# A hybrid decoder layer on one core: feed-forward in five token blocks, with the samples in the first superblock

## The chip, the cores and the metric

The kernel runs on one core of a Trainium2 chip. The metric is device time in microseconds (us) for one execution; before the change the median of three runs is 2588.84 us (2588.73 to 2595.58).

## What is computed

One layer of a decoder for 2048 prompt tokens and 8 x 8 = 64 sample tokens that share all weights. The model width is 1024, the hidden width of the feed-forward 4096, the memory has 256 tokens. All numbers are 32-bit floats.

```
h = rmsnorm(x) ; proj = h @ w_in             # q 512, k 128, v 128, u 512
attn = window attention, window 128, sinks, ALiBi (8 heads, 2 kv heads)
pool = causal means of u over 2, 4, 8, 16 tokens, times w_pool
x = x + concat(attn, pool) @ w_out
x = x + cross(rmsnorm(x) @ w_cq, mem_k, mem_v) @ w_co      # 4 heads x 256
x = x + square(relu(rmsnorm(x) @ w_up)) @ w_down
y = rmsnorm(x)
```

The prompt's memory keys and values come from `mem_prompt @ w_ck, w_cv`, and every prompt token shares them. Each of the 8 samples has its own window cache, pooling history and memory cache (`cmk`, `cmv`: 8 MB each), so the samples need an attention and a cross stage of their own.

## The kernel before, in words

Activations are kept transposed: channels on the 128 partitions, tokens along the free axis. Every product is made with three matmuls, because each operand is split into a rounded high part and a low part: Wh x Hh, Wh x Hl, Wl x Hh (`mm3`, L109 to L114, and the same three in `dense`, L310 to L312). A weight chunk of 128 x 1024 is loaded by a DMA of SyncE (SP) into one of six staging slots `f` (L132), rounded by ScalarE (L133), and its low part is made by VectorE (L134). The class `Stream` does this in the fixed order in which the chunks will be used, ahead of use, as long as there are pairs of the twelve weight slots `w` and staging slots left. Slots of every kind are handed out first in, first out, in the order of the program's text; the toolchain then plans the order of the instructions on each engine, which can differ from the text as far as the data and the slots allow. That order is fixed when the kernel is built.

The tokens are worked on in three superblocks of two blocks each (`SBLOCKS`, L24 to L28): 384 + 384, 384 + 384, and 256 + 320, where 320 is 256 prompt tokens and the 64 samples. `dense` takes each weight chunk through both blocks.

The prologue (L391) makes the prompt's memory keys and values and folds `w_cq` into the keys (`a_s`) and `w_co` into the values (`b_s`). Results of folds pass through the staging slots to DRAM (`put_fold`, L359). Each superblock (L513) then does:

- the input projection (L864), ten chunks of both blocks, in which `in_evac` (L544) splits keys and queries and makes the pooling sums. In the first superblock only, the four folds of `w_pool` into `w_out` (`fold`, L378) stand between its first four steps; they need `wpool`, loaded and scaled in `prep_fold` (L366), again through a staging slot;
- window attention, interleaved with the rest of the projection. Each tile of 128 tokens and each kv head pass five steps (`attn_a` to `attn_pv`, from L690). In the last superblock the samples' attention (`attn_sample`, L772) comes first. From its start, that superblock keeps two staging slots for the samples' value caches (`cvs`, L534); `v32` (L523) takes one in every superblock;
- the output projection (`add_evac`, L923), the cross stage (`cross`, L946), and the product with `b_s` (`add_evac2`, L1126). In the last superblock `sample_cross` (L1001) runs beside `cross`: queries with `w_cq`, scores against 16 key tiles (L1037), softmax, 16 value tiles (L1075), and `w_co`;
- the feed-forward: `up(g)` and `down(g)` for eight groups of 512 hidden channels, in order up 0, up 1, down 0, up 2, down 1 and so on. Around down(6) and down(7), the input norms of the next superblock's two blocks are made (`norm1`, L488), four staging slots each. After down(7), `final` (L1212) norms and stores a block.

Small pieces such as norms are put in a list (`later`) and taken up by `flush` a counted number of chunk steps later.

The keys of a superblock's last 128 tokens are carried to the next one in split form by GpSimd (`kcar`, L522 and L559).

Of the kernel before, what the change touches and what calls it, by code (L numbers as in the profile page):

```python
# [14 lines left out]
P = 128  # L15
NB = 384
# [16 lines left out]
C_D, C_DS, C_RC, C_QSC, C_SLS = 0, 256, 640, 704, 708  # L33
C_N = 710
# [17 lines left out]
def kernel(ctx: ExitStack, tc: tile.TileContext, io, nW=12, nF=6, nT=8):  # L52
# [10 lines left out]
    FS = Slots([sb(f"f{i}", 1088) for i in range(nF)])  # L63
    TS = Slots([sb(f"t{i}", 400) for i in range(nT)])
    XT = [sb(f"x{i}", 3136) for i in range(2)]
# [4 lines left out]
    b_s = drp.tile([8, P, 1024], F32, name="b_s", tag="b_s")  # L70

# [11 lines left out]
    kcar = sb("kcar", 512, F32R)  # L83
# [80 lines left out]
    for s in range(3):  # L164
        for c in CIN:
            S.add(("in", s, c), io["win"][c])
            if s == 0 and c in (0, 1):
                for g in range(2):
                    S.add(("wop", 2 * c + g), io["wop"][2 * c + g])
        for c in range(8):  # L170
            S.add(("wo", s, c), io["woa"][c], wo_s[c])
        for hf in range(2):
            for kp in range(4):
                S.add(("A", s, hf, kp), a_s[hf, kp])
        for c in range(8):
            S.add(("B", s, c), b_s[c])
        for g in range(9):
            for c in range(4):
                if g < 8:
                    S.add(("up", s, g, c), io["wup"][4 * g + c])  # L180
            for c in range(4):
                if g > 0:
                    S.add(("dn", s, g - 1, c), io["wdn"][4 * (g - 1) + c])
# [79 lines left out]
    def gain(bl, act, k, g):  # L263

        gk = vec[:, g + k:g + k + 1]
        nc.scalar.activation(act.hi(k), bl.x(k), AF.Copy, scale=gk)  # L266
        nc.vector.scalar_tensor_tensor(act.lo(k), bl.x(k), gk, f32(act.hi(k)), ALU.mult, ALU.subtract)

    class Act:
        def __init__(self, n):  # L270
            self.n = n
            self.h = [ACTS.get(), ACTS.get()]
            self.l = [ACTS.get(), ACTS.get()]

        def hi(self, k, c0=0, c1=None):
            return k4(self.h[k // 4])[:, k % 4, c0:self.n if c1 is None else c1]

        def lo(self, k, c0=0, c1=None):
            return k4(self.l[k // 4])[:, k % 4, c0:self.n if c1 is None else c1]
# [8 lines left out]
    def order(nch, head, tail):  # L288
        out = []
        for lo_, hi_, outer in ((0, head, True), (head, nch - tail, False), (nch - tail, nch, True)):  # L290
            if outer:
                out += [(c, b) for b in (0, 1) for c in range(lo_, hi_)]
            else:
                out += [(c, b) for c in range(lo_, hi_) for b in (0, 1)]
        return out

    def dense(keys, blks, hi, lo, evac, head=2, tail=3, after=None, piece=8, seq=None):
# [3 lines left out]
        for c, b in seq or order(nch, head, tail):  # L301
            while fetched <= c:
                loaded[fetched] = S.next(keys[fetched])
                left[fetched] = 2
# [4 lines left out]
            for k in range(8):  # L309
# [3 lines left out]
                if k < 7 and k % piece == piece - 1:  # L313
                    yield
            evac(c, b, ps)
# [50 lines left out]
    def prep_fold():  # L366
        wpr = WS.get()
        nc.sync.dma_start(cst[:], io["cst"])
# [107 lines left out]
    def make_blks(s):  # L476
        blks = []
        off = 0
        for b, (t0, npr, ns) in enumerate(SBLOCKS[s]):
            bl = Blk()  # L480
            bl.s, bl.b, bl.t0, bl.np, bl.ns, bl.n, bl.off = s, b, t0, npr, ns, npr + ns, off
            off += npr
            bl.xt = XT[b]
            bl.x = (lambda bl: lambda k, c0=0, c1=None: bl.xt[:, 0:8 * bl.n].rearrange("p (k n) -> p k n", n=bl.n)[:, k, c0:bl.n if c1 is None else c1])(bl)
# [3 lines left out]
    def norm1(bl, wait=2):  # L488
# [5 lines left out]
        else:  # L494
            xs = [FS.get() for _ in range(4)]
            for i in range(4):
                nc.sync.dma_start(xs[i][:, 0:2 * n], io["x"][:, 8 * bl.t0 + 2 * i * n:8 * bl.t0 + 2 * (i + 1) * n])
# [12 lines left out]
    def load_x(bl):  # L510
        nc.sync.dma_start(bl.xt[:, 0:8 * bl.n], io["x"][:, 8 * bl.t0:8 * (bl.t0 + bl.n)])

    def superblock(s, blks, nxt):  # L513
        last = s == 2
        smp = blks[1] if last else None
        npt = sum(bl.np for bl in blks)
        kz = [[WS.get() for _ in range(2)] for _ in range(2)]
        for kv in range(2):
            for hl in range(2):
                i = 2 * kv + hl  # L520
                if s > 0:
                    nc.gpsimd.tensor_copy(kz[kv][hl][:, 0:P], f32(kcar[:, i * P:i * P + P]))  # L522
# [6 lines left out]
        if last:  # L529
# [14 lines left out]
        def in_evac(c, b, ps):  # L544
            bl = blks[b]
            n = bl.n
            if c == 0:
                for kv in range(2):
                    r = slice(64 * kv, 64 * kv + 64)
                    o = slice(64 - 64 * kv, 128 - 64 * kv)  # L550
                    d = slice(P + bl.off, P + bl.off + bl.np)
                    src = ps[r, 0:bl.np]
                    rnd(src, kz[kv][0][r, d], kz[kv][1][r, d])
                    nc.scalar.copy(kz[kv][0][o, d], src)
                    nc.vector.tensor_tensor(kz[kv][1][o, d], src, f32(kz[kv][0][r, d]), ALU.subtract)
                    if b == 1 and not last:
                        for hl in range(2):
                            i = 2 * kv + hl
                            nc.gpsimd.tensor_copy(kcar[:, i * P:i * P + P], f32(kz[kv][hl][:, P + npt - P:P + npt]))  # L559
                if smp is bl:  # L560
                    t = TS.get()
                    nc.vector.tensor_copy(t[:, 0:192], ps[:, bl.np - P:n])
                    nc.sync.dma_start(io["wkp"], t[:, 0:P])
                    nc.sync.dma_start(io["wks"][:, :, 120:128], t[:, P:192].rearrange("p (b t) -> p b t", t=8))
                    for kv in range(2):
                        r = slice(64 * kv, 64 * kv + 64)
                        nc.gpsimd.tensor_copy(kS[r, kv, :], t[r, P:192])
                        nc.sync.dma_start(io["wks"][r, :, 0:120], ckz[r, :, kv, 8:P])
                    TS.put(t)
            elif c == 1:  # L570
                nc.vector.tensor_copy(v32[:, bl.off:bl.off + n], ps[:, 0:n])
                if smp is bl:
                    nc.sync.dma_start(io["wvp"], v32[:, npt - P:npt])
            elif c < 6:
                j = c - 2
                if last and (c, b) == (2, 0):
# [7 lines left out]
                if smp is bl:  # L584
                    nc.vector.tensor_scalar(
# [98 lines left out]
        cp = Slots(TS2)  # L684
# [87 lines left out]
        def attn_sample():  # L772
# [3 lines left out]
            dsm = cst[:, C_DS:C_DS + 384].rearrange("p (g s) -> p g s", s=192)  # L776
# [25 lines left out]
            TS.put(qf)  # L802
            nc.vector.tensor_scalar(t[:, 8:12], t[:, 0:4], -1.0, None, ALU.mult)
# [46 lines left out]
        if last:  # L850
# [25 lines left out]
        def attn():  # L876
# [11 lines left out]
            if last:  # L888
# [34 lines left out]
        def add_evac(c, b, ps):  # L923
            bl = blks[b]
            nc.vector.tensor_tensor(bl.x(c), ps[:, 0:bl.n], bl.x(c), ALU.add)  # L925
            gain(bl, bl.h2, c, V_GCROSS)
# [19 lines left out]
        def cross():  # L946
# [13 lines left out]
            for hf in range(2):  # L960
                A = [S.next(("A", s, hf, kp)) for kp in range(4)]
                for bl in blks:
# [23 lines left out]
                    if hf == 1:  # L986
                        bl.h2.free()
# [5 lines left out]
        def load_split(src):  # L993
            r, th, tl = FS.get(), ACTS.get(), ACTS.get()
            nc.sync.dma_start(r[:, 0:1024], src)
            nc.scalar.copy(th[:, 0:1024], r[:, 0:1024])
            nc.vector.tensor_tensor(tl[:, 0:1024], r[:, 0:1024], f32(th[:, 0:1024]), ALU.subtract)
            FS.put(r)
            return th, tl

        def sample_cross():  # L1001
            bl = smp
            q0, q1 = AUX.get(), AUX.get()
            qq = [q0, q1]
            for k in range(8):
                w = load_split(io["wcq"][k])
                for i in range(2):
                    mm3(qq[i][0:64, :], [k], lambda k: bl.h2.hi(k, bl.np, bl.n), lambda k: bl.h2.lo(k, bl.np, bl.n),
                        lambda k: w[0][:, 512 * i:512 * i + 512], lambda k: w[1][:, 512 * i:512 * i + 512], k == 0, k == 7)
                ACTS.put(*w)  # L1010
            yield
# [3 lines left out]
            AUX.put(q0, q1)  # L1015
            qt = AUX.get()
# [3 lines left out]
            qzc = [FS.get(), FS.get()]  # L1020
            for bg in range(2):
                nc.gpsimd.memset(qzc[bg][:, 0:1024], 0.0)
                qv = qzc[bg][:, 0:1024].rearrange("p (i x) -> p i x", x=P)
                for b in range(4):
                    nc.vector.tensor_copy(qv[:, :, 40 * b:40 * b + 8], qt[:].rearrange("p (i n) -> p i n", n=64)[:, :, 32 * bg + 8 * b:32 * bg + 8 * b + 8])
            AUX.put(qt)
            yield
            sp = AUX.get()
            for bg in range(2):
                qv = qzc[bg][:, 0:1024].rearrange("p (i x) -> p i x", x=P)  # L1030
                for b in range(4):
                    for hh in range(2):
                        kk = FS.get()
                        nc.sync.dma_start(kk[:, 0:1024], io["cmk"][4 * bg + b, hh])
                        for i in range(4 * hh, 4 * hh + 4):
                            h, db = i // 2, i % 2
                            nc.tensor.matmul(sp[32 * h:32 * h + 32, 256 * bg:256 * bg + 256], qv[:, i, 32 * b:32 * b + 32],  # L1037
                                             kk[:, 256 * (i % 4):256 * (i % 4) + 256], start=b == 0 and db == 0, stop=b == 3 and db == 1,
                                             tile_position=(0, 32 * h))
                        FS.put(kk)  # L1040
                    yield
            FS.put(*qzc)
# [9 lines left out]
            for g in range(2):  # L1052
                nc.gpsimd.tensor_scalar(pp[:, 256 * g:256 * g + 256], pp[:, 256 * g:256 * g + 256], t[:, 6 + g:7 + g], 1.0, ALU.mult, ALU.mult)
            st.put(t)
            ptz = [FS.get(), FS.get()]
            for bg in range(2):
                nc.gpsimd.memset(ptz[bg][:, 0:1088], 0.0)
# [316 lines left out]
```

## Time and profile before

| what | value |
|---|---|
| median of three runs | 2588.84 us |
| the profiled run | 2594.3 us |
| its span, first to last instruction | 2592.5 us |
| mean granted TensorE clock | 0.995 |
| 114 to 317 us | first superblock: input projection, attention, output projection |
| 460 to 926 us | inside the first superblock's feed-forward |
| 2020 to 2131 us | cross stages of the third superblock |
| DMA, all queues | 244.75 MB |

In the rows of the stages the columns are the window, its length, then the busy time and the number of instructions of PE (TensorE's matmuls), PEld (its weight loads), DVE (VectorE), ACT (ScalarE) and POOL (GpSimd), the granted clock, the share of the DMA engines' time, and GB/s. In rows of single instructions the first two numbers are start and duration. Rows of groups give the count, the busy time, the mean duration in ns, and the idle time before them with what ended it. Matmul records overlap, so a matmul's price is the distance from its start to the next one's.

### The profile page before, as it was taken

What the parts mean: (1) busy time and instruction counts of PE and PEld (TensorE: products, weight loads), DVE (VectorE), ACT (ScalarE), POOL (GpSimd) and SP (SyncE); (2) the same over time, 40 slices, a digit from 0 to 9 for tenths busy, and PEclk for the clock granted to TensorE, in tenths of its full rate; (3) what the DMA queues carried; (4) which work ended last, traced back from release to release, by engine and by line L of the source; (5) the groups of instructions that cost most, each with busy time, mean ns of one, the idle gap of its engine ahead of it and who ended that gap; (6) DMA issues with size and microseconds to landing.
All of it is one profiled execution on the core that took longest, in us unless ns stands there. A gap on an engine that the chain in (4) does not pass through costs nothing. (4 is left out here: it accounts for less than half of the span.)

```text
span 2592.5 us, 38981 instructions
## 1 busy us (share of the span) xinstructions
PE 2554.5 (99%) x15775; PEld 2459.0 (95%) x15775; DVE 1385.8 (53%) x2632; ACT 997.9 (38%) x1923; POOL 175.8 (7%) x298
## 2 busy tenths in 40 slices
PE   9899999999999999999999999999999999999998
PEld 8798989999999999998999999999999769999998
DVE  8568545434444367954454344445767446444444
ACT  6666343322222244843332222223456444322331
POOL 0015010000000001421000000000022010000000
PEclk9999999999999999999999999999999999999999
DMA  7833212221211123141111222112424573222210
GB/s 282 261 124 102 88 37 78 66 65 66 65 59 64 58 65 122 40 140 57 66 62 61 65 65 66 60 59 65 141 74 143 196 277 112 83 82 82 82 58 37
DMA packets 92538, 244.75 MB, mean 94 GB/s; under 512 B 16773, under 2 KB 31557, under 8 KB 91205
## 3 DMA queue, kind: packets, MB, share of 16 engines
q1 hardware_dynamic: 92356, 242.25, 28.4%
q8 instruction: 124, 2.03, 0.3%
q14 instruction: 58, 0.47, 0.1%
HBM read 219.53 MB, written 22.69 MB: 93 GB/s over the span
## 5 line engine op out<-in xcount | busy, mean ns | idle before, releaser
L310 PE MATMUL mm<-act,w 128*128 128x384 f32 (+2 forms) x2784 | 900.4, 323 | 1.7 <-ACT act L664 1.6
L312 PE MATMUL mm<-act,w 128*128 128x384 f32 (+2 forms) x2784 | 895.8, 322 | 1.0 <-DVE w L134 0.9
L311 PE MATMUL mm<-act,w 128*128 128x384 f32 (+2 forms) x2784 | 895.9, 322 | 0.7 <-DVE act L665 0.5
L133 ACT CAST w<-f 128x1024 fp32r<-128x1024 f32 x330 | 346.0, 1050 | 828.9 <-PE mm L113 499.0
L112 PE MATMUL mm<-act,w 128*128 128x384 f32 (+2 forms) x1728 | 552.4, 320 | 3.6 <-DVE t L417 2.4
L114 PE MATMUL mm<-act,w 128*128 128x384 f32 (+2 forms) x1728 | 548.8, 318 | 1.4 <-DVE w L134 1.4
L113 PE MATMUL mm<-act,w 128*128 128x384 f32 (+2 forms) x1728 | 548.6, 317 | 0.0
L310 PEld LDWEIGHTS mm<-act,w 128*128 128x128 f32 x2784 | 525.9, 189 | 5.9 <-ACT act L664 1.9
L311 PEld LDWEIGHTS mm<-act,w 128*128 128x128 f32 x2784 | 525.8, 189 | 5.9 <-issue 2.1
L312 PEld LDWEIGHTS mm<-act,w 128*128 128x128 f32 x2784 | 525.6, 189 | 2.1 <-DVE w L134 1.8
L134 DVE TENSOR_TENSOR w<-f,w 128x1024 fp32r<-128x1024 f32 x330 | 402.7, 1225 | 129.4 <-ACT w L133 127.4
L1199 DVE TENSOR_TENSOR x<-mm,x 128x384 f32<-128x384 f32 (+2 forms) x384 | 200.0, 522 | 326.4 <-PE mm L114 326.4
L112 PEld LDWEIGHTS mm<-act,w 128*128 128x128 f32 x1728 | 327.1, 189 | 5.3 <-issue 2.6
L114 PEld LDWEIGHTS mm<-act,w 128*128 128x128 f32 x1728 | 326.9, 189 | 1.8 <-DVE w L134 1.8
L113 PEld LDWEIGHTS mm<-act,w 128*128 128x128 f32 x1728 | 326.9, 189 | 1.1
L1165 DVE SCALAR_TENSOR_TENSOR t<-mm,t 128x384 f32<-128x384 f32 (+1 forms) x192 | 100.6, 524 | 285.7 <-PE mm L312 285.7
L1166 ACT ACTIVATE t<-t 128x384 f32<-128x384 f32 (+1 forms) x192 | 95.0, 495 | 251.4 <-DVE t L1165 251.4
L1169 DVE TENSOR_TENSOR act<-t,act 128x384 fp32r<-128x384 f32 (+1 forms) x192 | 100.1, 521 | 103.9 <-ACT act L1168 103.9
L112 PE MATMUL mm<-w,act 128*128 128x512 f32 x288 | 115.0, 403 | 1.9 <-ACT w L133 1.8
L113 PE MATMUL mm<-w,act 128*128 128x512 f32 x288 | 113.6, 395 | 1.6 <-DVE w L134 1.6
L114 PE MATMUL mm<-w,act 128*128 128x512 f32 x288 | 113.3, 394 | 0.0
L266 ACT ACTIVATE act<-x,vec 128x384 fp32r<-128x384 f32 (+2 forms) x96 | 56.3, 587 | 111.1 <-DVE x L925 57.5
(200 smaller groups left out, 2040.6 us busy)
## 6 DMA issues: line engine op xcount, KB each, us to landing
f<-in_wup SPq DMA_DIRECT2D x96, 512.0 KB, 3.5
f<-in_wdn SPq DMA_DIRECT2D x96, 512.0 KB, 3.4
f<-in_win SPq DMA_DIRECT2D x30, 512.0 KB, 3.7
f<-a_s SPq DMA_DIRECT2D x24, 512.0 KB, 4.2
f<-b_s SPq DMA_DIRECT2D x24, 512.0 KB, 4.3
x<-in_x SPq DMA_DIRECT2D x6, 1536.0 KB, 7.7
f<-in_wco SPq DMA_DIRECT2D x16, 512.0 KB, 5.4
f<-in_cmk SPq DMA_DIRECT2D x16, 512.0 KB, 4.5
```

What stands on the lines that cost most here:

```text
L112: nc.tensor.matmul(ps, Wh(k), Hh(k), start=first and i == 0, stop=False)
L113: nc.tensor.matmul(ps, Wh(k), Hl(k), start=False, stop=False)
L114: nc.tensor.matmul(ps, Wl(k), Hh(k), start=False, stop=final and i == last)
L133: nc.scalar.copy(th[:], r[:, 0:1024])
L134: eng.tensor_tensor(tl[:], r[:, 0:1024], f32(th[:]), ALU.subtract)
L310: nc.tensor.matmul(ps[:, 0:n], w8(th)[:, k, :], hi(b, k), start=k == 0, stop=False)
L311: nc.tensor.matmul(ps[:, 0:n], w8(th)[:, k, :], lo(b, k), start=False, stop=False)
L312: nc.tensor.matmul(ps[:, 0:n], w8(tl)[:, k, :], hi(b, k), start=False, stop=k == 7)
L1165: nc.vector.scalar_tensor_tensor(r[:, 0:n], ps[:, 0:n], 0.0, bl.r3[:, 0:n], ALU.max, ALU.mult)
L1166: nc.scalar.activation(q[:, 0:n], r[:, 0:n], AF.Square)
L1169: nc.vector.tensor_tensor(lo, q[:, 0:n], f32(hi), ALU.subtract)
L1199: nc.vector.tensor_tensor(bl.x(m), ps[:, 0:n], bl.x(m), ALU.add)
```

## The change

The superblocks are now 256 + 320, 384 + 384, 384 + 384, with the samples in the first. In its feed-forward, the first superblock takes both its blocks' 512 prompt tokens as one block (`FB`), so 512 columns per matmul; up to there, and in the cross stage, its blocks stay 256 and 320 wide. The 64 samples do not go through that feed-forward. Their cross stage is a generator (`side`) of which one step is taken after each of the 64 chunk steps of that feed-forward; it takes `w_cq` and `w_co` from the common stream, one key or value tile a step, each loaded one step ahead. Its result goes to DRAM (`x_s`), and 16 samples are added to each of the four later blocks when these load `x`: their feed-forward and final norm are 400 wide. The feed-forward thus runs in five blocks of 512, 400, 400, 400 and 400 tokens.

With it go: keys are carried in unsplit form by VectorE and split again at the next superblock's start (`put_k`), on ScalarE and VectorE; the copies of h2 that `side` reads are made by GpSimd; the number of staging slots stays six (1024 columns for 1088), that of weight slots twelve; in the first superblock the next input norms start one flush after their loads instead of two, and both its blocks' `final` come after the last step of down(7).

```diff
-    [(0, 384, 0), (384, 384, 0)],
-    [(768, 384, 0), (1152, 384, 0)],
-    [(1536, 256, 0), (1792, 256, 64)],
+    [(0, 256, 0), (256, 256, 64)],
+    [(512, 384, 0), (896, 384, 0)],
+    [(1280, 384, 0), (1664, 384, 0)],
 ]
+NS = 16
+SO = 46
...
+    SIDE = {**{k: ("sq", k) for k in range(8)}, **{SO + k: ("so", k) for k in range(8)}}
...
+                        if s == 0 and step in SIDE:
+                            n2, k = SIDE[step]
+                            S.add((n2, k), io["wcq" if n2 == "sq" else "wco"][k])
+                        step += 1
...
+        def put_k(src, kv, d):
+            r = slice(64 * kv, 64 * kv + 64)
+            o = slice(64 - 64 * kv, 128 - 64 * kv)
+            rnd(src, kz[kv][0][r, d], kz[kv][1][r, d])
+            nc.scalar.copy(kz[kv][0][o, d], src)
+            nc.vector.tensor_tensor(kz[kv][1][o, d], src, f32(kz[kv][0][r, d]), ALU.subtract)
...
-        last = s == 2
-        smp = blks[1] if last else None
+        last, has = s == 2, s == 0
+        smp = blks[1] if has else None
...
-        if last:
+        if has:
+            ds_ = cp.get()
+            nc.sync.dma_start(ds_[:, 0:384], io["cst"][:, C_DS:C_ALL])
...
+            for j in range(16):
+                fetch("cmk", j + 1)
...
+                kk = ahead.popleft()
...
+            for j in range(4):
+                nc.sync.dma_start(x_s[j], bl.xv[:, :, bl.np + NS * j:bl.np + NS * j + NS])
...
-        if last:
-            mix(cross(), sample_cross(), 1, 2)
-        else:
-            run(cross())
+        run(cross())
+        side = sample_cross() if has else iter(())
...
+            if not has or bl.b == 0:
+                fb = FB()
+                fb.parts, fb.n = [], 0
+                fbs.append(fb)
+            bl.fb, bl.fo = fb, fb.n
+            fb.parts.append(bl)
+            fb.n += bl.nf
...
         def up(g):
-            run(dense([("up", s, g, c) for c in range(4)], blks,
...
+            for _ in dense([("up", s, g, c) for c in range(4)], fbs,
...
+                           head=2 if g == 0 else 0, tail=0, early=has and g == 0):
+                next(side, None)
...
-            norm1(nxt[0])
+            norm1(nxt[0], 1 if has else 2)
         down(6)
         if nxt is not None:
-            norm1(nxt[1])
+            norm1(nxt[1], 1 if has else 2)
         down(7)
+        run(side)
```

More of the change, by code (lines that the diff above doesn't have):

```diff
@@ L15 @@
 P = 128
-NB = 384
+NB = 400
 SEQ = 2048
@@ L286, with order @@
         pass
-    def order(nch, head, tail):
+    class FB:
+        pass
+    def order(nch, head, tail, nb=2):
         out = []
@@ L1026, in sample_cross, with fetch @@
             AUX.put(qt)
+            ahead = deque()
+            def fetch(name, i):
+                if i < 16:
+                    t = FS.get()
+                    nc.sync.dma_start(t[:, 0:1024], io[name][i // 2, i % 2])
+                    ahead.append(t)
+            fetch("cmk", 0)
             yield
             sp = AUX.get()
[L1029 to L1041, printed above, removed]
```

324 lines of the change are left out of this document (178 added, 146 removed).

## The prediction

> **What bounds the kernel now.** I read the page first, then the busy time by stage, then single matmuls in order of time.
>
> ```profile
> span 2592.5 us, 38981 instructions
> PE 2554.5 (99%) x15775; PEld 2459.0 (95%) x15775; DVE 1385.8 (53%) x2632; ACT 997.9 (38%) x1923; POOL 175.8 (7%) x298
> ```
>
> ```profile
> 460.00:926.00 466.00, 466.00 (x2689) 465.73 (x2688) 192.26 (x287) 125.78 (x193) 0.00 (x0) 1.00 0.20 63
> 926.00:992.00 66.00, 66.00 (x377) 65.20 (x376) 54.32 (x104) 27.71 (x52) 1.40 (x4) 1.00 0.29 93
> 992.00:1120.00 128.00, 125.77 (x756) 119.02 (x755) 108.16 (x278) 84.23 (x212) 45.97 (x64) 1.00 0.27 93
> 1183.00:1330.00 147.00, 146.68 (x771) 133.49 (x770) 71.91 (x128) 58.62 (x119) 11.18 (x24) 1.00 0.19 62
> 2020.00:2131.00 111.00, 109.22 (x704) 73.86 (x702) 47.05 (x104) 41.84 (x80) 12.26 (x22) 1.00 0.69 241
> ```
>
> TensorE is the bound nearly everywhere. Busy time cannot show whether it runs at its full rate, because records overlap; the distance between starts can. In the feed-forward (460 to 926) 2689 matmuls of 384 columns take 466 us, 0.1733 us each, without a gap. For other widths I take first and last starts of unbroken runs:
>
> ```profile
> 2179.73 0.28 PE L310 MATMUL mm<-act,w 128*128 128x256 f32 x1
> ...
> 2182.25 0.31 PE L310 MATMUL mm<-act,w 128*128 128x320 f32 x1
> ...
> 2185.78 0.28 PE L310 MATMUL mm<-act,w 128*128 128x256 f32 x1
> ```
>
> ```profile
> 1190.01 0.39 PE L113 MATMUL mm<-w,act 128*128 128x512 f32 x1
> ...
> 1194.32 0.39 PE L114 MATMUL mm<-w,act 128*128 128x512 f32 x1
> ```
>
> 21 matmuls of 256 lie between the first two rows: 0.120 us each; then 24 of 320: 0.147; 19 of 512: 0.227. All four widths fit 0.417 ns a column plus a fixed 13.3 ns. So a token block less saves one fixed part per matmul, and gaps outside the feed-forward are what can be lost.
>
> **Part 1, five blocks for six.** A block has 1536 feed-forward matmuls (up 32 chunks x 8 x 3, down 64 x 4 x 3). Before, one of each block costs 4 x 0.1733 + 0.120 + 0.147 = 0.960 us. After, one of 512 and four of 400 (13.3 ns + 400 x 0.417 ns = 0.180): 0.947. 1536 x 0.0133 = **-20.5 us**, all on the path, since these stages have no gaps. Nothing else gets cheaper: the in, out and cross stages keep their six blocks and widths, only in another order. Evacuation in the wide block is two VectorE pieces of 256 per chunk; with the split of a weight it stays far under the 24 x 0.227 = 5.4 us of a step.
>
> The Trainium skill, page "TensorE: Matmul & The Clock Gate", section "Back-to-back issue gap", gives a warm matmul N/2.4 ns plus about 2.5 ns. By it this part would be worth 1536 x 2.5 ns = 3.8 us, an estimate; the rows above differ, and I go by them.
>
> **Part 2, the sample cross stage moved.** It ran beside the cross stage of the third superblock; now it runs one step per chunk in the first feed-forward. TensorE is full in both places, so its work is only carried over.
>
> ```profile
> L1037 PE MATMUL aux<-f,f 128*32 128x256 f32 x128 | 11.6, 384 | 0.4 <-DMA f<-in_cmk 0.4
> L1075 PE MATMUL aux<-f,f 128*32 128x256 f32 x128 | 9.4, 388 | 1.2 <-DMA f<-in_cmv 1.2
> ```
>
> ```profile
> 2075.23 1.06 PE L1037 MATMUL aux<-f,f 128*32 128x256 f32 x8
> 2076.22 0.50 PE L113 MATMUL mm<-w,act 128*128 128x512 f32 x1
> 2076.56 0.39 PE L114 MATMUL mm<-w,act 128*128 128x512 f32 x1
> ...
> 2092.36 0.64 PE L1075 MATMUL aux<-f,f 128*32 128x256 f32 x8 [1.19 <-DMA f<-in_cmv]
> 2092.93 0.50 PE L114 MATMUL mm<-w,act 128*128 128x512 f32 x1
> ```
>
> A single key tile (eight records, two heads) takes 2076.22 - 2075.23 = 0.99 us, a value tile (four heads) 0.57. One tile per step makes 16 x 0.99 = 15.8 us of keys for 11.6, and 9.1 of values for 9.4: +4. The matmul after each of the 32 groups takes 0.34 for 0.227: +3.5. Against that, the old stage goes: of the 111 us, 288 matmuls of 512 make 65.4, about 98 of 256 11.8, keys and values 21, transposes about 6: some 7 us are lost there. In the second superblock, without samples, 288 x 0.227 + 425 x 0.1733 + 48 transposes at about 0.11 leave 2.7 of 147 lost, so for two thirds of its tiles 1.8: -5. Together **+2** (bounds -3 and +10, the latter if the tiles, fetched only one step ahead, came late). The weight splits are as many as before; they now lie in the stream.
>
> **Part 3, the opening of the first superblock.** This is the dearest new thing. Weights, the pooled-weight matrix and the fold results all pass through the six staging slots `f`, handed out in turn. The next view is the DMA queue of SyncE, then TensorE.
>
> ```profile
> 122.32 0.34 SPq L370 DMA_DIRECT2D f<-in_wpool  x1
> 122.76 0.38 SPq L132 DMA_DIRECT2D f<-in_win  x1
> 123.23 0.38 SPq L132 DMA_DIRECT2D f<-in_wop  x1
> 127.50 0.93 SPq L363 DMA_DIRECT2D wo_s<-f  x2
> 130.78 0.34 SPq L132 DMA_DIRECT2D f<-in_wop  x1
> 131.73 0.91 SPq L363 DMA_DIRECT2D wo_s<-f  x2
> 135.49 0.34 SPq L132 DMA_DIRECT2D f<-in_win  x1
> ```
>
> ```profile
> 113.96 0.34 PE L310 MATMUL mm<-act,w 128*128 128x384 f32 x1
> ...
> 125.54 0.50 PE L112 MATMUL mm<-w,w 128*128 128x512 f32 x1 [2.71 <-ACT w L373]
> ...
> 141.73 0.33 PE L310 MATMUL mm<-act,w 128*128 128x384 f32 x1
> ```
>
> ```profile
> L133 ACT CAST w<-f 128x1024 fp32r<-128x1024 f32 x330 | 346.0, 1050 | 828.9 <-PE mm L113 499.0
> L134 DVE TENSOR_TENSOR w<-f,w 128x1024 fp32r<-128x1024 f32 x330 | 402.7, 1225 | 129.4 <-ACT w L133 127.4
> ...
> f<-in_win SPq DMA_DIRECT2D x30, 512.0 KB, 3.7
> ...
> wo_s<-f SPq DMA_DIRECT2D x8, 256.0 KB, 3.8
> ```
>
> Four chunk steps and four folds lie between 113.96 and 141.73: 27.8 us for 96 x 0.1733 + 24 x 0.227 = 22.1 of work. Already now `wpool` waits for a slot until 122.32, and loads follow slots. The change takes two more slots here (`cvs`, the sample value caches, 1 MB) ahead of `wpool`; with `v32` three are held until the sample attention is done, and three go round. By the order of gets and puts, the slot of `wpool` passes to the second input chunk, and the slot of the first fold result passes in turn to the third pool-output row, the fourth, and the third input chunk. Each load holds it for 3.7 + 1.05 + 1.23 = 6.0 us. `wpool` lands behind 1 MB more, at about 127 (125.1 before); the first fold result is away at about 132; three times 6.0 gives 150 for the third input chunk, where TensorE was at 141.7. The four steps are also 96 x 0.1733 - 48 x (0.120 + 0.147) = 3.8 us shorter here (that work returns later), so the loss grows by 8.5 + 3.8, with about 1 for a longer idle gap: **+13**. Lower bound 0 (the planner finds other work or an earlier load; a gain has no mechanism), upper bound +18.
>
> **Part 4, the rest.** Sample attention moves along with the narrow blocks, at its old price, and the third superblock gets the shape of the second: 0. Where the first superblock meets the second, down(6) and down(7) last 8 x 5.44 = 43.5 us for 66, while VectorE keeps both input norms. Its 54.3 + 108.2 = 162.5 us over 194 (84%) become:
>
> ```profile
> L1199 DVE TENSOR_TENSOR x<-mm,x x384: 410/557/558, 526.7 to 2581.8; 128x384 f32<-128x384 f32 x128, 128x256 f32<-128x256 f32 x32, 128x320 f32<-128x320 f32 x32
> L1216 DVE SCALAR_TENSOR_TENSOR x<-x,vec,t x48: 479/609/619, 989.3 to 2588.6; 128x384 f32<-128x384 f32 x32, 128x320 f32<-128x320 f32 x8, 128x256 f32<-128x256 f32 x8
> ```
>
> 32 residual adds at 0.410 for 0.557, 14 norm adds likewise, 16 final scalings at 0.479 for 0.609: 9 less; the key carry, now on ScalarE and VectorE: 1.5 more. 155 over 171.5 is 90%. Bounds 0 (only order) and +13 (84% again: 184.5); I take **+4**, nearer to zero, as the norms can start early.
>
> The tail: the last scalings and adds are 400 wide for 256.
>
> ```profile
> 2581.42 0.74 DVE L1199 TENSOR_TENSOR x<-mm,x 128x256 f32<-128x256 f32 x2
> ...
> 2585.84 3.25 DVE L1216 SCALAR_TENSOR_TENSOR x<-x,vec,t 128x256 f32<-128x256 f32 x8
> ```
>
> About a dozen VectorE steps in chain, each 0.15 us longer, and some 0.4 us on the other engines, less 0.7 for which the add now waits behind the other block's scalings: **+1.5**.
>
> **Sum:** -20.5 + 2 + 13 + 4 + 1.5 = 0. The profiled run took 2594.3 us, 1.8 beside its span and 5.5 above the median of 2588.84; the difference is applied to the median: **2589 us**. About 0.3%, 7.8 us, can be told from no change.
>
> **The rivals.**
> Faster: the opening and the seam stay hidden, because loads reach their slots earlier than my chain has them. For it: `wpool` is late by 2.7 us only. Against it: the chain is one slot's reuse, which no order can shorten. -20.5 + 2 + 1.5 + about 4 = -13: 2576. Chance 0.33.
> Slower: VectorE becomes the bound at the seam. It decides as soon as the two input norms run into the second superblock's evacuations, that is if VectorE cannot exceed its 84%: +13 for +4 makes 2598; with the upper bound of the opening, 2603. For it: 90% is above any stretch quoted. Against it: feed-forward stretches before it leave VectorE idle. Chance 0.25.
> Slower, by a smaller fixed part: the weight load of each matmul lies beneath its neighbour; if it is that which holds back the narrow widths, and wide matmuls of the feed-forward's operands (the 512 row has activations stationary) gain only a fifth of the 13.3 ns, the first part saves 4 and the time is 2606. The rule of the Trainium skill in "TensorE: Matmul & The Clock Gate", section "Back-to-back issue gap", would come out there too. The straight line through 256, 320 and 384, with the very operands of the feed-forward, speaks against it: 0.03.
> My forecast, gain and new losses cancelling: 0.39.
>
> **How the numbers follow.** Faster 0.33, same 0.39, slower 0.28. The range goes from 2574, just past the first rival, to 2604, past the second; what lies outside is a gain without losses (-19) and both upper bounds with the last rival.
>
> **What would show it.** Steps right: feed-forward starts 0.227 apart in the wide block and 0.180 in the others; third input chunk of the first superblock near 150 us; key groups of 0.99 us among them. Wrong: that chunk near 140, or gaps in the first feed-forward at `cmk`/`cmv` loads, or gaps of over 10 us in all after the first seam.

## The result and the profile after

The changed kernel takes **2626.74 us** (median of 4 runs, 2626.09 to 2627.73) against 2588.78 (2586.76 to 2595.58) for the kernel before on the same chip: ratio **1.0142, 95% interval 1.0124 to 1.0161**. It is slower by 38 us, outside the predicted range. Its profiled run took 2626.8 us with a span of 2624.9, 32.4 more than the span of the profiled run before (which lay 5.5 above its own median). The top of the page after:

```profile
span 2624.9 us, 35890 instructions
PE 2569.3 (98%) x14239; PEld 2396.3 (91%) x14239; DVE 1382.9 (53%) x2646; ACT 989.9 (38%) x1931; POOL 174.2 (7%) x300
```

TensorE has 1536 matmuls fewer, as the change meant it to have, and is busy for 15 us more. That contradiction is the first thing to explain, and busy time cannot do it. The stages can, each from its first matmul to the first of the next (us, worked out from the matmuls' starts; "in" holds the input projections and the attention, "cross" the cross scores and their projection). A feed-forward is counted here, and below, to the start of its last group of three matmuls, which leaves out 0.5 to 0.7 us ahead of the next superblock; the tail runs from there to the end of the span:

| stage | before: 1st, 2nd, 3rd superblock | after | after less before, sum |
|---|---|---|---|
| prologue | 114.0 | 111.0 | -3.0 |
| in | 132.1, 123.5, 108.8 | 136.9, 132.3, 123.6 | +28.4 |
| output projection | 71.1, 67.6, 53.6 | 54.8, 68.5, 69.5 | +0.5 |
| cross | 139.6, 139.6, 146.3 | 95.6, 141.6, 141.6 | -46.7 |
| feed-forward | 534.5, 534.2, 414.1 | 407.3, 561.9, 564.4 | +50.8 |
| tail | 12.4 | 15.0 | +2.5 |

The superblocks have other sizes now, so only sums compare. The samples' cross stage has left the cross column and entered the feed-forward one, so these two belong together: +4.1, where the prediction had -20.5 + 2. The stretch of the second superblock's feed-forward after, in the view of busy time by stage (length, TensorE busy and its records, clock, DMA share, GB/s), corresponds to the 460 to 926 row of before:

```profile
1160.00:1660.00 500.00, 500.00 (x2744) 1.00 0.19 61
```

500 us for 2744 matmuls are 182.2 ns each, at a full clock and without a gap. The prediction's line gives 180.0 for 400 columns.

The rows that follow name lines of the changed kernel: L115 to L117 and L325 to L327 are the matmuls, L136 and L137 make the high and the low part of a weight, L388 and L391 load and scale the pooling weights, L571 loads the value caches, L1252 is the residual add, L1080 a key tile's matmuls.

The opening of the first superblock: the waits of TensorE between 110 and 160 us (waiting line, releaser, us, times, longest), the DMA queue of SyncE, and the first matmul of the third input chunk:

```profile
PE mm L115 <- ACT w L391: 7.4, 1, 7.4
PE mm L325 <- ACT w L136: 4.0, 2, 3.1
PE mm L327 <- DVE w L137: 1.7, 3, 0.8
```

```profile
117.71 1.91 SPq L571 DMA_DIRECT2D f<-in_cvz  x2
119.71 0.39 SPq L388 DMA_DIRECT2D f<-in_wpool  x1
...
126.70 0.33 SPq L135 DMA_DIRECT2D f<-in_win  x1
...
144.22 0.82 SPq L135 DMA_DIRECT2D f<-in_win  x2
```

```profile
148.92 0.41 PE L325 MATMUL mm<-act,w 128*128 128x320 f32 x1 [3.06 <-ACT w L136]
```

The loads of the value caches stand ahead of `wpool`, and the third chunk is loaded at 144.2 and used at 148.9: the predicted chain, with the predicted 150.

The seam to the second superblock: TensorE's waits from 800 to 830 us, busy time by stage on both sides of it (TensorE, weight loads, VectorE, ScalarE, GpSimd, then the clock), SyncE's loads of the next input weights and VectorE's splits of them:

```profile
PE mm L327 <- DVE w L137: 4.8, 1, 4.8
PE mm L325 <- DVE x L1252: 1.0, 1, 1.0
```

```profile
780.00:807.00 27.00, 27.00 (x119) 21.85 (x117) 25.42 (x57) 17.07 (x34) 0.00 (x0) 1.00 0.39 129
807.00:835.00 28.00, 22.20 (x110) 21.50 (x111) 22.06 (x46) 9.29 (x18) 0.65 (x3) 0.88 0.41 139
```

```profile
792.91 24.82 SPq L135 DMA_DIRECT2D f<-in_win  x9
```

```profile
812.71 4.63 DVE L137 TENSOR_TENSOR w<-f,w 128x1024 fp32r<-128x1024 f32 x4
```

VectorE is 94% busy ahead of the seam, then TensorE stands still and four splits come in a row. This picture fits two causes: VectorE is full, or the splits were asked for too late. The clock column shows a second cost: from 814 to 819 us TensorE is working again, busy for all 5 us, and its granted clock is 0.50.

The samples' key tiles inside the first feed-forward, TensorE in order of time:

```profile
490.31 0.39 PE L327 MATMUL mm<-act,w 128*128 128x512 f32 x1
490.63 1.06 PE L1080 MATMUL aux<-f,x 128*32 128x256 f32 x8
491.63 0.50 PE L325 MATMUL mm<-act,w 128*128 128x512 f32 x1
491.97 0.40 PE L326 MATMUL mm<-act,w 128*128 128x512 f32 x1
```

The group is 1.00 us long, as priced. But it costs on both edges: the matmul ahead of it takes 0.32 us to the group's start and the one behind it 0.34, each for 0.227.

### The profile page after: what moved, and what is told of

It is laid out like the page before. It is cut to its first block, busy times and chain, and to the rows that moved or that the text cites. A ratio compares the mean times of both kernels' runs of the same rounds, so it can differ in the third digit from the quotient of the medians.

```text
span 2624.9 us, 35890 instructions
## 1 busy us (share of the span) xinstructions
PE 2569.3 (98%) x14239; PEld 2396.3 (91%) x14239; DVE 1382.9 (53%) x2646; ACT 989.9 (38%) x1931; POOL 174.2 (7%) x300
## 4 chain that ended last, share of the span: by engine, by line
PE 88%; DVE 4%; ACT 3%; DMA 2%; POOL 2%; issue 1%; SPq 0%; DVEq 0%; ACTq 0%; POOLq 0%
PE mm L327 16%; PE mm L325 16%; PE mm L326 16%; PE mm L115 12%; PE mm L117 12%; PE mm L116 12%; DVE w L137 1%; PE aux L739 1%; POOL t L658 1%; DMA f<-in_wco 1%; ACT x L751 1%; PE aux L770 1%; ACT w L136 1%; PE aux L1080 1%; PE aux L984 1%
## 5 line engine op out<-in xcount | busy, mean ns | idle before, releaser
L325 PE MATMUL mm<-act,w 128*128 128x400 f32 (+4 forms) x2528 | 863.7, 342 | 6.0 <-ACT w L136 4.0
L327 PE MATMUL mm<-act,w 128*128 128x400 f32 (+4 forms) x2528 | 859.4, 340 | 8.5 <-DVE w L137 8.5
L326 PE MATMUL mm<-act,w 128*128 128x400 f32 (+4 forms) x2528 | 860.5, 340 | 0.0
L136 ACT CAST w<-f 128x1024 fp32r<-128x1024 f32 x346 | 363.2, 1050 | 910.6 <-PE mm L116 501.9
L115 PE MATMUL mm<-act,w 128*128 128x400 f32 (+2 forms) x1472 | 509.1, 346 | 4.0 <-DVE t L435 2.3
L117 PE MATMUL mm<-act,w 128*128 128x400 f32 (+2 forms) x1472 | 509.6, 346 | 1.9 <-DVE w L137 1.9
L116 PE MATMUL mm<-act,w 128*128 128x400 f32 (+2 forms) x1472 | 507.2, 345 | 0.0
L325 PEld LDWEIGHTS mm<-act,w 128*128 128x128 f32 x2528 | 478.3, 189 | 27.6 <-ACT w L136 7.4
L327 PEld LDWEIGHTS mm<-act,w 128*128 128x128 f32 x2528 | 480.7, 190 | 20.2 <-DVE w L137 9.6
L326 PEld LDWEIGHTS mm<-act,w 128*128 128x128 f32 x2528 | 478.4, 189 | 11.7
L137 DVE TENSOR_TENSOR w<-f,w 128x1024 fp32r<-128x1024 f32 x346 | 422.6, 1226 | 114.1 <-ACT w L136 105.9
L1252 DVE TENSOR_TENSOR x<-mm,x 128x400 f32<-128x400 f32 (+1 forms) x384 | 195.1, 521 | 348.8 <-PE mm L117 346.3
L115 PEld LDWEIGHTS mm<-act,w 128*128 128x128 f32 x1472 | 276.4, 188 | 22.7 <-issue 3.7
L117 PEld LDWEIGHTS mm<-act,w 128*128 128x128 f32 x1472 | 277.9, 189 | 13.6 <-DVE w L137 2.3
L116 PEld LDWEIGHTS mm<-act,w 128*128 128x128 f32 x1472 | 276.3, 188 | 10.1
L1216 DVE SCALAR_TENSOR_TENSOR t<-mm,t 128x400 f32<-128x400 f32 (+1 forms) x192 | 97.8, 523 | 344.5 <-PE mm L327 344.4
L1217 ACT ACTIVATE t<-t 128x400 f32<-128x400 f32 (+1 forms) x192 | 91.8, 493 | 215.1 <-DVE t L1216 215.1
L1220 DVE TENSOR_TENSOR act<-t,act 128x400 fp32r<-128x400 f32 (+1 forms) x192 | 97.4, 520 | 76.6 <-ACT act L1219 76.5
L115 PE MATMUL mm<-w,act 128*128 128x512 f32 x288 | 114.9, 402 | 3.2 <-ACT w L136 1.7
L117 PE MATMUL mm<-w,act 128*128 128x512 f32 x288 | 113.1, 393 | 0.0
L272 ACT ACTIVATE act<-x,vec 128x384 fp32r<-128x384 f32 (+3 forms) x96 | 56.4, 588 | 118.2 <-DVE x L956 61.0
```

Source lines behind the costliest of these rows:

```text
L115: nc.tensor.matmul(ps, Wh(k), Hh(k), start=first and i == 0, stop=False)
L116: nc.tensor.matmul(ps, Wh(k), Hl(k), start=False, stop=False)
L117: nc.tensor.matmul(ps, Wl(k), Hh(k), start=False, stop=final and i == last)
L136: nc.scalar.copy(th[:], r[:, 0:1024])
L137: eng.tensor_tensor(tl[:], r[:, 0:1024], f32(th[:]), ALU.subtract)
L325: nc.tensor.matmul(ps[:, 0:n], w8(th)[:, k, :], hi(b, k), start=k == 0, stop=False)
```

## The experiments

What I held after reading the two traces: the loss has four separate places. The matmuls are slower because the rows of the activation tensors moved from 384 to 400 columns apart (**layout**); the opening loses to the value caches' slots; the seam loses to late splits; the samples' steps lose at their edges. The rivals were one common bound (VectorE or the DMA queue) or the new order of work. The kernel before took 2590.8 to 2593.3 us as a median beside these runs, so the verdict on an edit is read from the length of its stage, with the time beside it.

**Matmuls alone.** No diff: groups of 24 matmuls in the kernel's order, at several widths and distances between rows.

> This kernel leaves out the whole layer and runs only groups of 24 matmuls (128x128 weights, the order high-high, high-low, low-high over eight rows), 144 of them for each of 17 combinations of width and of the distance from one row to the next in the moving tensor, nothing else beside them on any engine. Layout theory (the spacing of a matmul depends on where its moving rows lie, not only on its width): 384 columns with rows 384 apart 173 ns each, the same 384 columns with rows 400 apart 175 to 177 ns; 400 columns with rows 400 apart 182 ns, and between 179 and 181 ns at one of the distances 416, 448 or 512. Rival one (the width alone, with the neighbours of the whole kernel as the disturbance): 384 columns 173 ns at both distances, and 400 columns one number at every distance. Rival two (the clock or traffic in the changed kernel, not the instruction): 173 and 180 ns throughout here, where nothing else runs.

TensorE, the second group's first row and the last row of four cases; 119 matmuls lie between each two. In turn: 384 columns with rows 384 apart, 384 with rows 400 apart, 400 with rows 400 apart, 400 with rows 512 apart.

```profile
50.95 0.33 PE L85 MATMUL q<-act,w 128*128 128x384 f32 x1
...
71.58 0.33 PE L87 MATMUL q<-act,w 128*128 128x384 f32 x1
...
76.05 0.33 PE L85 MATMUL q<-act,w 128*128 128x384 f32 x1
...
97.00 0.34 PE L87 MATMUL q<-act,w 128*128 128x384 f32 x1
...
101.66 0.34 PE L85 MATMUL q<-act,w 128*128 128x400 f32 x1
...
123.35 0.34 PE L87 MATMUL q<-act,w 128*128 128x400 f32 x1
...
180.38 0.34 PE L85 MATMUL q<-act,w 128*128 128x400 f32 x1
...
201.80 0.34 PE L87 MATMUL q<-act,w 128*128 128x400 f32 x1
```

20.63, 20.95, 21.69 and 21.42 us over 119: 173.4, 176.1, 182.3 and 180.0 ns. Nothing else runs and the granted clock is 1.00, so both rivals fall. The 180.0 of the prediction's line exists, but at rows 512 (or 448) apart; 416 apart gave 182.2 like 400. At 256 columns it went the other way (120.0 with 384, 118.3 with 400), and 320 did not move (146.7 both).

**The kernel before with rows 400 apart, and its control.**

```
-NB = 384
+NB = 400
```

> The kernel before with only the rows of its activation tensors moved from 384 to 400 columns apart; blocks, order and samples stay. To make room some buffers are packed otherwise, which its control does as well. Layout theory: every 384-wide matmul that reads such rows takes 2 to 3 ns more, some 10,000 of them, so 18 to 26 us slower than the control, 2608 to 2615. Rival (the loss comes with the new order of work): no more than 2 us from the control.

> Control of the one above: the kernel before with the same packing of its small buffers and its rows still 384 apart. All theories: 2588, within 3 us of the kernel before.

2609.1 us (ratio to the kernel before 1.0068, 1.0053 to 1.0083) against 2592.62 for the control (1.0002, 0.9993 to 1.0012): **16.5 us for the layout alone**, a little under the expected 18 to 26; the 256-wide matmuls gain: the third superblock's feed-forward went from 414.1 to 409.0, the first's from 534.5 to 543.0. The stretch of 460 to 926 us, the kernel with 400 first, its control second:

```profile
460.00:926.00 466.00, 466.00 (x2646) 465.73 (x2645) 188.46 (x279) 120.91 (x183) 0.00 (x0) 1.00 0.18 62
```

```profile
460.00:926.00 466.00, 466.00 (x2691) 466.00 (x2690) 193.71 (x290) 125.94 (x194) 0.00 (x0) 1.00 0.18 62
```

Both are busy for all 466 us. Only the count of records tells them apart: 45 fewer matmuls were done in the same time.

**The changed kernel with rows of up to 384 columns 384 apart.**

```
-    def k4(t, n=NB):
-        return t[:, 0:4 * NB].rearrange("p (k n) -> p k n", n=NB)[:, :, 0:n]
+    def k4(t, n=384):
+        return t[:, 0:4 * 384].rearrange("p (k n) -> p k n", n=384)[:, :, 0:n]
...
-            self.w = NB if n <= NB else 512
+            self.w = 384 if n <= 384 else NB if n <= NB else 512
```

> The changed kernel with the rows of all activation tensors of at most 384 columns 384 apart again; only the 400-wide feed-forward of the second and third superblock keeps 400. Layout theory: the 384-wide groups of input, output, combined and last cross projections win 2.8 ns a matmul, the cross scores some 4, together 8 to 11 us, 2616 to 2619. Rival (the width or the order of work): 2626, within 2 us.

2619.59 us (1.0111, 1.0091 to 1.0131), span 2615.8: 7 us back by the median and 9 by the span, for the 8 to 11 that the layout theory gave (its four runs lie between 2613.8 and 2622.4). The cross stages of the second and the third superblock are 139.6 again, for 141.6.

**Weights of the seam loaded early.**

```
-        S.resF = 4 if nxt is not None else 0
+        S.resF = 0 if nxt is None or has else 4
+        if has:
+            S.resW = 4
```

> The changed kernel in which the last two down-projections of the first superblock no longer keep four staging slots free: the weights of the second superblock's first input projections may be loaded and split as soon as a slot and a pair of weight buffers is free (four buffers kept for the keys). Theory (the 1.2 and 5.0 us that TensorE stands still at 806.7 and 808.9 us come from splits that start late because of the reservation): both gone, 5 to 7 us faster, 2620 to 2622. Rival (VectorE is the bound there, 95% busy over 780 to 817 us, and splits that start earlier only push its other work later): 0 to 2 us, 2625 to 2627, with the same idle time of TensorE behind another wait on VectorE.

2618.07 us (1.0096, 1.0081 to 1.0111); "in" of the second superblock 123.5 for 132.3, **8.8 us**, the length it had before the change, and more than the 5 to 7 expected. The first input weights are loaded 8.4 us earlier, and no wait of TensorE is left from 800 to 835 us:

```profile
784.53 32.73 SPq L135 DMA_DIRECT2D f<-in_win  x9
```

```profile
780.00:807.00 27.00, 27.00 (x119) 22.14 (x119) 26.32 (x59) 17.37 (x36) 0.00 (x0) 1.00 0.33 118
807.00:835.00 28.00, 28.00 (x159) 27.82 (x158) 26.40 (x56) 12.61 (x25) 0.65 (x3) 1.00 0.51 172
```

VectorE is busier than in the changed kernel, 97% ahead of the seam and 94% behind it, and costs nothing. So it was not the bound; the reservation of four staging slots was, and the rival falls. The expectation had priced the waits alone, 5.8 us. The granted clock, 1.00 here and 0.88 in the same row of the changed kernel, accounts for most of the rest: 5 us of work at 0.50 lose an estimated 2.5 us. (The four weight buffers that the edit keeps free instead are those that the next superblock's keys take.)

**The sample values loaded after the folds.**

```
-            cvs = [FS.get(), FS.get()]
-            for i in range(2):
-                nc.sync.dma_start(cvs[i][:, 0:1024], io["cvz"][:, 1024 * i:1024 * (i + 1)])
...
+        if has:
+            for i in range(2):
+                c = FS.get()
+                cvs.append(c)
+                nc.sync.dma_start(c[:, 0:1024], io["cvz"][:, 1024 * i:1024 * (i + 1)])
...
         S.resW = RW
```

> The changed kernel in which the two staging slots for the samples' cached values, and their two loads, are taken after the four folds instead of at the first superblock's start. Theory (the opening loses some 10 us because the pooling weights and the first input chunks queue for staging slots that the values hold): TensorE's 7.6 us at 117.8 us shrink to under 3, the third input chunk is used before 145 us, 7 to 11 us faster, 2616 to 2620. Rival (the loss there is the samples' added work in the first attention, or traffic on the queue whatever holds the slots): 0 to 3 us.

2613.56 us (1.0085, 1.0067 to 1.0103); "in" of the first superblock 125.3 for 136.9 and its output projection 53.2 for 54.8: **13.2 us**, more than the 7 to 11 expected. SyncE's queue, TensorE's wait for the pooling weights, and the third input chunk's first matmul:

```profile
119.66 0.35 SPq L388 DMA_DIRECT2D f<-in_wpool  x1
120.11 0.39 SPq L135 DMA_DIRECT2D f<-in_win  x1
...
133.69 3.67 SPq L135 DMA_DIRECT2D f<-in_win  x3
...
143.59 2.73 SPq L906 DMA_DIRECT2D f<-in_cvz  x2
```

```profile
PE mm L115 <- ACT w L391: 4.8, 1, 4.8
```

```profile
140.53 0.39 PE L325 MATMUL mm<-act,w 128*128 128x256 f32 x1 [1.46 <-ACT w L136]
```

The load of `wpool` starts no earlier (119.66 for 119.71), and TensorE still waits 4.8 us for it, not under 3: here only the megabyte ahead of it is gone. The larger part comes with the slots, as predicted: the second chunk is loaded 6.6 us earlier, the third at 133.7 for 144.2, and used 8.4 us earlier. The granted clock is higher as well, 0.93 from 110 to 160 us, where it was 0.86 in the changed kernel and 0.97 in the kernel before.

**Two tiles to a step.** The old cross stage had taken two tiles at a time; this undoes the "small steps" of the change, and puts the heads in turn. The cut shows the key tiles; the value tiles are paired likewise, and as there are 16 steps fewer, `w_co` stands 16 steps sooner in the stream.

```
-            for j in range(16):
-                fetch("cmk", j + 1)
+            for j in range(0, 16, 2):
...
-                for i in range(4 * hh, 4 * hh + 4):
+                for i in (0, 2, 4, 6, 1, 3, 5, 7):
...
+                fetch("cmk", j + 2)
+                fetch("cmk", j + 3)
```

> The changed kernel in which the samples' cross stage inside the first feed-forward takes two key tiles, or two value tiles, to a step: eight matmuls of all four heads instead of four, and 16 steps fewer. The next two tiles are fetched once the two are used, so no more slots are held. Theory (each step costs its switch, some 0.3 us, and a key tile's four matmuls of two heads take 0.99 us where a value tile's of four heads take 0.57): 16 switches by 0.3 us and 16 tiles by 0.4 us, 9 to 12 us faster, 2615 to 2618. Rival one (matmuls of the four heads do not run side by side, only switches are saved): 4 to 5 us, 2622. Rival two (the fetches then come late): no faster, and TensorE waits for a key tile.

2609.63 us (1.0068, 1.0053 to 1.0083); the first feed-forward 394.8 for 407.3: **12.5 us**, just over what both parts of the theory give, so both rivals fall. By the starts of the groups, 16 x 0.99 us of keys and 16 x 0.57 of values became 16 x 1.00, 9.0 less, and 16 pairs of edges went. The time fell by 17, more than the 9 to 12 expected; what is more than the stage's 12.5 is spread over places that the edit does not touch, by at most 1.2 us each (14.9 in the span), and over what single executions differ by. TensorE in order of time:

```profile
489.75 0.39 PE L327 MATMUL mm<-act,w 128*128 128x512 f32 x1
490.07 1.07 PE L1080 MATMUL aux<-f,x 128*32 128x256 f32 x16
491.07 0.50 PE L325 MATMUL mm<-act,w 128*128 128x512 f32 x1
```

Two key tiles (16 records, four heads) take the 1.00 us that one (8 records, two heads) took. The Trainium skill, page "TensorEngine Tiling (Array Packing)", section "Key Properties", says that tiles work in parallel and that changing the tiling mode drains TensorE. The trace agrees with the first: 16 records in the time of 8. At the edges it shows a loss, 0.09 us ahead of each of the 32 groups of the changed kernel and 0.11 us behind; that this is a drain no run here shows.

**The four together.** No new edit.

> The changed kernel with the four edits together: rows 384 apart outside the feed-forward, the seam's loads free, the values late, two tiles to a step. If the four losses are separate places on TensorE's path they add: 7 (measured) + 6 + 9 + 10 = 32 us, 2594, and up to 2600 where one of them hides another. Rival (one common bound, VectorE or the DMA queue, behind all of them): over 2608.

2585.77 us (0.9979, 0.9970 to 0.9988), better than expected; the rival of one common bound falls. The four spans taken back one by one are 9.1 + 8.7 + 12.8 + 14.9 = 45.5 us; together they give 40.7 (2624.9 - 2584.3), so they are separate places but for 5 us. Of these, 1.8 are counted twice, since the layout edit also shortened "in" of the second superblock (130.5 for 132.3) and the seam edit alone already brings it to 123.5, the four together to 123.3; and 2.5 lie in the prologue (113.5 for 111.0), whose length went from 110.2 to 113.5 us over these runs; why stays open.

**Where rows begin.** A second kernel of matmuls alone.

> This kernel too leaves out the whole layer and only runs groups of 24 matmuls, 96 for each case. First two rows in turn, the second 0 to 56 columns behind a multiple of 64, widths 400, 384 and 256; then the kernel's own pattern at 400 columns in rows 400 apart with the low rows turned by 0 to 3 places in their tile, with the eight rows taken in order or 0, 4, 1, 5, 2, 6, 3, 7, and with the low row second or third of its three matmuls; last the cross scores' 512-wide matmul with its weights read from rows 384 or 400 apart. Theory (what counts is where a row begins against where the last one was, in columns modulo 64): with both rows on multiples of 64 the line of the run before, 180 ns at 400 and 173 at 384; with other distances up to 8 ns more or less, the same for all pairs of one distance, and one of the sixteen orders of the pattern within 0.5 ns of 180 or below. Rival one (a row that does not begin on a multiple of 64 costs 2 ns whatever came before): 182 in all sixteen orders, and 182 where both rows begin 16 columns behind a multiple. Rival two (the pitch itself): two rows in turn show the line at every distance. For the weights read from rows 400 apart: 231 ns if the loss of the cross scores is theirs, 227 if not.

Each row is one case of 96 matmuls of 400 columns: two rows in turn on multiples of 64 columns; the kernel's pattern; the same with the low rows two places further in their tile.

```profile
49.87 17.53 PE L78 MATMUL q<-act,w 128*128 128x400 f32 x96
...
424.40 17.74 PE L78 MATMUL q<-act,w 128*128 128x400 f32 x96
...
459.56 17.63 PE L78 MATMUL q<-act,w 128*128 128x400 f32 x96
```

0.21 and 0.10 us over 95 distances: 2.2 and 1.1 ns a matmul above the first case, which from first to last group runs at 180.0. Among the two-row cases the second row 8, 16, 32 or 40 columns off gave 183.3, 181.7, 181.6 and 180.8; among the sixteen patterns the values lay between 180.9 and 182.4. So rivals one and two fall: neither a fixed price for a row off the multiples of 64 nor the pitch explains these; the same rows in another order cost another time. My own rule in its simple form falls as well. Both rows 16 off: 180.0, as it should be; but both 32 or both 48 off: 183.4, though their distance is a multiple of 64; and no order of the pattern came within 0.5 ns of 180.0. Which addresses meet badly stays open. The cross scores' matmul, with its weights read from rows 384 and 400 apart, took 226.7 and 231.7 ns: that part of the cross stages' 2 us is the weights' layout, not the moving rows'.

**The four and the low rows turned.**

```
         def lo(self, k, c0=0, c1=None):
-            return self.at(self.l, k, c0, c1)
+            return self.at(self.l, k ^ 2 if self.w == NB else k, c0, c1)
```

> The kernel of the four edits with one more: in the 400-wide feed-forward the low rows lie two places further in their tile (row k in place k exclusive-or 2), nothing else. Theory (the spacing follows where the rows begin; the pattern alone measured 181.0 ns so, 182.2 as they lay): 6,144 matmuls by 1.15 ns, 7 us faster, 2579; the feed-forward of the second and the third superblock 3.5 us shorter each, 558 and 561 us. Rival (in the whole kernel evictions and loads beside the matmuls hide or change this): no more than 2 us, 2584 to 2586.

**2581.91 us, ratio 0.9960 (0.9947 to 0.9974)**, faster than both kernels. The feed-forward of the second and the third superblock took 558.5 and 561.1, for 561.9 and 564.4: 3.4 and 3.3 us, the forecast to a tenth or two. The span fell by 5.1 and not 7, since "in" of the first superblock, which the edit does not touch, took 126.1 for 123.0 in this execution. The stretch that took 2744 matmuls in the changed kernel:

```profile
1160.00:1660.00 500.00, 500.00 (x2759) 1.00 0.19 63
```

## Why the prediction was wrong, step by step

**Part 1, the 400-wide price (13.3 ns + 400 x 0.417 ns = 0.180): failed in its size.** The mechanism holds: a block less saves one fixed part of 13.3 ns per matmul, and the line through 256, 320, 384 and 512 meets 180.0 at 400 where rows lie well. But all four widths of the line had been measured with rows 384 or 512 columns apart, and the diff changes that distance (`NB = 400` is also the pitch). 1536 x (0.227 + 4 x 0.1822 - 0.960) = -6.5 us where -20.5 was forecast: 14 us gone.

**"Nothing else gets cheaper: the in, out and cross stages keep their six blocks and widths": it got dearer.** Their widths stayed and their layout did not: 9.1 us by the span, 7 by the median, given back when only the rows were put 384 apart again. This term stood at nothing because I costed instructions by their shapes, and a shape does not show where its rows begin.

**Part 2, the samples moved (+2): right sort, undersized.** The feed-forward pays 407.3 - 1536 x 0.227 = 58.6 us for them; the cross stages give up 425.5 - 374.7 = 50.8 (before against the version with rows 384 apart, 95.5 + 139.6 + 139.6). +7.8, within the bounds to +10, though not by late tiles as those had it. I priced only the matmul behind a group (0.11 us), and the one ahead of it loses 0.09 as well: the key groups start 6.70 us apart (490.63 and 497.33), for 24 x 0.227 = 5.45 and the group's 1.00, so an edge pair costs 0.25. 32 of them cost 8.0 us, of which I had priced 3.5: that explains 4.5 of the 5.8 us that are missing. About 1 more are the norms' matmuls (L222) in this stretch, which the 58.6 counts in; the rest stays open.

**Part 3, the opening (+13): right** in mechanism and in its landmark (third chunk at 148.9 for 150), and close in size (13.2 given back when the two slots are taken later). Some luck is in it. The pooling weights were there at 125.0 and not at 127, because the prologue ended 3.0 us earlier, and no term named the granted clock. Some 4 us are open: with the slots taken late, "in" and the output projection of the first superblock still take 125.3 + 53.2 = 178.5, where the narrow superblock of before took 108.8 + 53.6 = 162.4 and coming first cost 12.1 there (203.2 for 191.1).

**Part 4, the seam (+4): the place was right, the cause was not.** It cost 8.8 us, waits of 5.8 and the lower clock behind them, and I had derived it from VectorE's share of 90%. With its splits asked for early VectorE ran at 97% without a wait. What stopped TensorE was a line that I had not followed, `S.resF = 4` ahead of the last two down-projections. It reserves four of the six staging slots, and while the first norm of the next superblock holds four itself, no weight is loaded ahead. The line stood in the kernel before, too; that it did no harm there because those two projections lasted 66 us and not 43.5 is argued, not tried. The rival "slower by VectorE at the seam" falls with it. The tail cost 2.5 for 1.5.

The sum of what was measured, -6.5 + 9 + 7.8 + 13 + 8.8 + 2.5 = +34.6, stands against +32.4 between the spans. Of the 2 us between, 1.8 are the part of the second superblock's "in" that both the layout and the seam count; the prologue's -3.0 and the 4 us that are open in the opening stand in no term and nearly cancel. The first rival (opening and seam hidden) was wrong in both. The last rival gave a smaller fixed part of a matmul; the fixed part is whole, and what is lost comes from elsewhere. By the rule of the Trainium skill in "TensorE: Matmul & The Clock Gate", section "Back-to-back issue gap" (N/2.4 plus 2.5 ns, there for an isolated matmul and not for a stream with weight loads), a 400-wide matmul would take an estimated 169.2 ns; this case shows 180.0 at best.

## What to carry to other kernels

A price per instruction, taken from a trace, holds for its shape and for its addresses: when an edit changes a tile's width, ask what distance between rows goes with it, and count instructions in a stretch of full busy time before and after, because a busy share cannot show a slower rate. When buffers are handed out in turn, a new early holder delays everything that comes round through its slot, and a reservation that was harmless in a long stage can starve the next one when the stage gets shorter. A high busy share is a suspicion, not a bound: take away the late request first, and see whether the engine can go higher. And read the granted clock behind a wait: here waits of 5.8 us cost 8.8.

## What the runs showed of the hardware

The spacing of fp32r matmuls of equal width varied by up to 3.4 ns with the place of their moving rows alone: at 400 columns 180.0 (rows on multiples of 64 columns) to 183.4, at 384 173.3 to 176.7, while at 256 other places were faster than these (116.7 to 120.0). Reading the weights from rows 400 apart slowed a 512-wide matmul from 226.7 to 231.7 ns. Two groups of column-tiled fp32 matmuls on four column groups took the 1.00 us that one on two took. After the longer wait at the seam (4.8 us, TensorE at work again from 814.0) the granted clock was 0.50 up to 819 us; without the wait it was 1.00 there.
